# Inverting the triangles of a gated DeltaNet: 32-wide substitution against 16-wide substitution and one more block level

## The chip, the cores and the metric

The kernel runs on one core of a Trainium2 chip. The metric is the time of one execution in microseconds, as the device takes it. Of the kernel before there are three runs: 3832.81 us in the median, from 3832.29 to 3837.66.

## The reference

Two layers of a trunk run over 1024 latent and 256 context tokens of width 1024. In each, one input projection feeds three groups of heads: four gated DeltaNet (GDN) heads of width 128, run forwards and backwards over the tokens; a bidirectional linear recurrence (RG-LRU); and four heads of latent attention (MLA). One output projection and an MLP of squared ReLU follow. All data are fp32. The part that the change touches is in the GDN heads:

```python
def gdn_chunked(q, k, v, g, beta, s0):
    ...
    low = jnp.where(strict, jnp.einsum('nbhid,nbhjd->nbhij', kb, k) * decay, 0.0)
    amat = low + jnp.eye(GDN_CHUNK, dtype=low.dtype)
    rhs = jnp.concatenate([v * beta[..., None], kb * jnp.exp(G)[..., None]], axis=-1)
    sol = lax.linalg.triangular_solve(amat, rhs, left_side=True, lower=True, unit_diagonal=True)
    u, w = sol[..., :dv], sol[..., dv:]
    attn = jnp.einsum('nbhid,nbhjd->nbhij', q, k) * decay
    ...
    def step(S, inp):
        u_i, w_i, a_i, qg_i, kg_i, gl_i = inp
        v_new = u_i - jnp.einsum('bhcd,bhde->bhce', w_i, S)
        o_i = jnp.einsum('bhcd,bhde->bhce', qg_i, S) + jnp.einsum('bhij,bhje->bhie', a_i, v_new)
        S = S * gl_i[..., None, None] + jnp.einsum('bhcd,bhce->bhde', kg_i, v_new)
        return S, o_i
    S, o = lax.scan(step, s0, (u, w, attn, qg, kg, glast))
```

For every chunk of tokens a unit lower triangular matrix (`low` plus the identity) has to be solved. Only then can the scan, which goes from chunk to chunk, start.

## The kernel before

Tokens are kept along the free dimension, channels on the 128 partitions. Every large product of a weight and an activation is taken as three products of halves (high and low part of each, `mm3`, L230), 128 rows by up to 512 columns. The weights come by DMA as `wr` (SyncE's queue) and are split into `wh` (ScalarE) and `wl` = `wr` - `wh` (GpSimd, through the helper `tt`, L138). The helpers `act` (L135), `tt` (L138), `ts` and `stt` (L147) issue most other operations, so these lines stand for many places of the program; names of tiles tell them apart.

`mixer` writes the work of one layer in this order: `tiles(h)` for a head h (the projections to its k, q, v and z, with a convolution and a transposition, L443 and L462, behind each), `head(h)` (the GDN head), so that the projections of head h+1 are written behind head h, with a few tiles of the other groups between. After `head(2)` come the last projections, then `head(3)`; beside that one there is no projection left, and `mla_open`, `mla_prep` and `mla_attend` (the attention) and `lru` (the recurrence) are written behind it. What an engine does next is decided when the program is built: the Tile scheduler makes a list for each engine from the order of the program (the priority), the dependencies and its own estimates of times. So a part that gets shorter also changes which work stands between its instructions. At run time each engine goes through its list strictly in order, and waits on semaphores of the others.

The GDN head works with 10 chunks of 128 tokens (`NCH`) in two directions. `gdn_head` reads k, q and v back by DMA, forms the decays (L624, L636, L646) and the triangles `N[0]` and `N[1]`, each 128 x 10 x 128: minus the strictly triangular part, one lower, one upper. `gdn_invert` then inverts all 20 of them in place:

1. The four diagonal blocks of 32 x 32 of each triangle are brought together in `C` (128 x 20 x 32, four bands of partitions): direction 0 by four copies (L658), direction 1 transposed by 40 products with the identity on TensorE (L676) and a copy. `C` is filled up to 32 blocks with zeros by GpSimd (L668).
2. VectorE transposes in blocks of 32 (L681) to `X`, where each partition holds one whole 32 x 32 block along its free dimension, and sets the diagonal to one (L682).
3. The substitution: in 30 steps j, VectorE multiplies column j below the diagonal with row j left of it (`T`, r x j elements, r = 31 - j) and adds the product to `X`. That makes 60 operations on 9,920 elements per partition, each waiting for the one before. All blocks of a head are inverted at once, on 80 of 128 partitions.
4. Two block transposes (L689, L690) give the inverses back, as `X1` (in the place of `C`) and transposed as `X2`.
5. Two levels of block recursion on TensorE join 32 to 64 and 64 to 128 (products of L696, with copies between PSUM and SBUF that alternate between VectorE and ScalarE, `cp2`, L658).

`gdn_scan` follows (L766 to L790), then `gdn_y`, which scales the output on ScalarE and transposes it on TensorE (L821). `C`, `X` and `X2` are used again by the scan as buffers. PSUM is shared out in tags of one bank each: a, b and c serve the GDN head, d and st the convolutions and the attention, two banks of mm and one of lr the projections.

Of the kernel before, what the change touches and what calls it, by code (L numbers as in the profile page):

```python
# [7 lines left out]
F32 = mybir.dt.float32  # L8
# [3 lines left out]
ALU = mybir.AluOpType  # L12
# [4 lines left out]
P = 128  # L17
# [5 lines left out]
NCH = TOK // P  # L23
# [20 lines left out]
class Trunk:  # L44
# [615 lines left out]
    def gdn_invert(self, N):  # L660

        nc = self.nc
        C = self.g5("C")[:, 0:1024].rearrange("p (q i) -> p q i", i=32)
        X = self.g5("X")[:, 0:1024].rearrange("p (q i) -> p q i", i=32)
        X2 = self.g5("X2")[:, 0:1024].rearrange("p (q i) -> p q i", i=32)
        nc.gpsimd.memset(C[:, 2 * NCH:, :], 0.0)  # L668
        for a in range(4):
            q = slice(32 * a, 32 * a + 32)  # L670
            self.cp2(a, C[q, 0:NCH, :], N[0][q, :, 32 * a:32 * a + 32])
        pc = self.PT('a').rearrange("p (c i) -> p c i", i=32)
        for a in range(4):
            q = slice(32 * a, 32 * a + 32)
            for c in range(NCH):
                nc.tensor.matmul(pc[q, c, :], N[1][q, c, 32 * a:32 * a + 32], self.ident[q, 32 * a:32 * a + 32],  # L676
                                 start=True, stop=True, tile_position=(32 * a, 32 * a))
        self.act(C[:, NCH:2 * NCH, :], pc[:, 0:NCH, :])
        t = self.T()
        Xf = X.rearrange("p i j -> p (i j)")  # L680
        nc.vector.transpose(Xf, C.rearrange("p q i -> p i q"))  # L681
        nc.vector.memset(Xf[:, 0:1024:33], 1.0)  # L682
        for j in range(1, 31):
            r = 31 - j
            tv = t[:, 0:r * j].rearrange("p (i k) -> p i k", k=j)
            self.tt(tv, X[:, j + 1:32, j:j + 1].to_broadcast([P, r, j]), X[:, j:j + 1, 0:j].to_broadcast([P, r, j]), ALU.mult)
            self.tt(X[:, j + 1:32, 0:j], X[:, j + 1:32, 0:j], tv, ALU.add)
        X1 = C
        nc.vector.transpose(X1.rearrange("p q i -> p i q"), Xf)  # L689
        nc.vector.transpose(X2.rearrange("p q j -> p j q"), X.rearrange("p i j -> p j i"))  # L690
        Y = [[X1[:, 0:NCH], X2[:, 0:NCH]], [X2[:, NCH:2 * NCH], X1[:, NCH:2 * NCH]]]
        Q = [slice(32 * a, 32 * a + 32) for a in range(4)]
        H = [slice(0, 64), slice(64, 128)]

        def mm(out, lhsT, rhs, r, c):
            nc.tensor.matmul(out, lhsT, rhs, start=True, stop=True, tile_position=(r, c))  # L696

        pairs = [[(0, 1), (2, 3)], [(1, 0), (3, 2)]]
        pa = self.PT('b').rearrange("p (c i) -> p c i", i=32)
        for c in range(NCH):  # L700
            for d in range(2):
                for a, b in pairs[d]:
                    mm(pa[Q[b], c, :], N[d][Q[a], c, Q[b]], Y[d][1][Q[a], c, :], 32 * a, 32 * b)
        PT = self.T()[:, 0:320].rearrange("p (c i) -> p c i", i=32)
        self.act(PT, pa[:, 0:NCH, :])
        k = 0
        for d in range(2):
            for a in range(4):
                self.cp2(k, N[d][Q[a], :, Q[a]], Y[d][0][Q[a], :, :])
                k += 1  # L710
            for e in pairs[d][d]:
                self.cp2(k, self.XAT[Q[e], :, 32 * e - 64 * d:32 * e - 64 * d + 32], Y[d][1][Q[e], :, :])
                k += 1
        pw = self.PT('c').rearrange("p (c i) -> p c i", i=32)
        px = self.PT('a').rearrange("p (c i) -> p c i", i=32)
        for c in range(NCH):
            for d in range(2):
                for a, b in pairs[d]:
                    mm(pw[Q[a], c, :], PT[Q[b], c, :], Y[d][0][Q[b], c, :], 32 * b, 32 * a)
                a, b = pairs[d][d]  # L720
                mm(px[Q[b], c, :], Y[d][0][Q[b], c, :], PT[Q[b], c, :], 32 * b, 32 * b)
        for d in range(2):
            for a, b in pairs[d]:
                self.cp2(a, N[d][Q[a], :, Q[b]], pw[Q[a], 0:NCH, :])
            a, b = pairs[d][d]
            self.cp2(d, self.XAT[Q[b], :, 32 * a - 64 * d:32 * a - 64 * d + 32], px[Q[b], 0:NCH, :])

        for k in range(2):
            pb = self.PT('ab'[k]).rearrange("p (c i) -> p c i", i=64)
            for c in range(5 * k, 5 * k + 5):  # L730
                for d in range(2):
                    mm(pb[H[1 - d], c - 5 * k, :], N[d][H[d], c, H[1 - d]], self.XAT[H[d], c, :], 64 * d, 64 * (1 - d))
            PB = self.T()[:, 0:320].rearrange("p (c i) -> p c i", i=64)
            self.cp2(k, PB, pb[:, 0:5, :])
            pe = self.PT('cb'[k]).rearrange("p (c i) -> p c i", i=64)
            for c in range(5 * k, 5 * k + 5):
                for d in range(2):
                    mm(pe[H[d], c - 5 * k, :], PB[H[1 - d], c - 5 * k, :], N[d][H[1 - d], c, H[1 - d]], 64 * (1 - d), 64 * d)
            for d in range(2):
                self.cp2(d, N[d][H[d], 5 * k:5 * k + 5, H[1 - d]], pe[H[d], 0:5, :])  # L740

    def gdn_scan(self, h, gv, kT, ktd, vt, Y, at, Qg, last):

        nc = self.nc
        kt = self.g5("C").rearrange("p (c d) -> p c d", d=P)
        nc.sync.dma_start(kt, ktd.rearrange("p (c d) -> p c d", d=P))
        o = self.g5("X").rearrange("p (c d) -> p c d", d=P)
        sm = self.g5("X2").rearrange("p (k d) -> p k d", d=P)
# [189 lines left out]
    def mla_prep(self, L, h, mp, with_ctx):  # L938
# [35 lines left out]
        for b in qbl:  # L974
# [5 lines left out]
            for i in range(w):  # L980
                for j, b2 in enumerate(kb):
                    n2 = BLK[b2][1]
                    pm = self.G()[:, :n2]
                    nc.tensor.matmul(pm, a[0:96, 0, i * P:(i + 1) * P], K[b2][0:96, 0, :], start=True, stop=True)
                    nc.vector.tensor_reduce(mx[:, i, j:j + 1], pm, axis=AX.X, op=ALU.max)
            m1 = self.small([P, 4], "mx1", 2)
# [48 lines left out]
    def mixer(self, L, hs, obl):  # L1035

        nc = self.nc
# [6 lines left out]
        d = pk["krba"] = self.dram("krba")  # L1044
        ba = sp.tile([P, NCH, 16], F32, name=self.nm("ba"))
# [20 lines left out]
        gp = self.gp = self.pool("gp", other)  # L1066
        self.XAT = gp.tile([P, NCH, 64], F32, name=self.nm("XAT"))
        nc.gpsimd.memset(self.XAT, 0.0)
        kd, xg = [], []

        def tiles(h):
# [367 lines left out]
```

## Time and profile before

| what | value |
| --- | --- |
| median of the runs | 3832.81 us (3832.29 to 3837.66) |
| the profiled execution's own time | 3833.43 us |
| its span in the trace | 3831.6 us |
| instructions | 51,475 |
| TensorE's mean granted clock | 0.958 |
| ScalarE busy | 1645.2 us (43%) |
| GpSimd busy | 1310.3 us (34%) |
| moved by DMA | 347.13 MB, 91 GB/s |

The profile is of one execution. "Busy" is the time in which an engine executes something; PE is TensorE's matmuls, PEld its weight loads (which overlap), DVE VectorE, ACT ScalarE, POOL GpSimd. PEclk is the granted clock of TensorE as a share of full speed. A group's row names line, engine, operation, output and inputs, the shape, and behind "x" the count. A row of the timeline has start and duration in us, then the same, and in brackets the idle time ahead of it with what ended it. There are eight inversions, four per layer. By the trace they run, from the first block transpose to the first product after the substitution, from 174.4 to 219.4, 339.9 to 388.1, 485.5 to 525.4 and 630.5 to 691.5 us in layer 0, and from 2227.1 to 2273.4, 2379.7 to 2428.5, 2510.7 to 2559.9 and 2635.2 to 2696.2 us in layer 1.

### The profile page before, as it was taken

Reading aid. Unit: us, or ns where it says so; the run is one execution under the profiler, and the core shown is the slowest. Engines: PE = TensorE matmul, PEld = TensorE weight load, DVE = VectorE, ACT = ScalarE, POOL = GpSimd, SP = SyncE. Lnnn points to the kernel's source line nnn. Section 1 sums busy time; section 2 is a strip of 40 time slices with the busy share of each in tenths; the row PEclk is TensorE's granted clock in tenths of the full one; section 3 lists DMA queues with packets and bytes.
Section 4 is the critical chain, followed back from the end, with each engine's and each line's share of the span. In section 5 each row is a group of like instructions: output and inputs, shape, how many; then the busy total and the mean of one; then the engine's idle time right before and its main releaser. Section 6 shows DMA issues by size and latency. Waiting matters only on the chain. (4 is left out here: it accounts for less than half of the span.)

```text
span 3831.6 us, 51475 instructions
## 1 busy us (share of the span) xinstructions
PE 3501.0 (91%) x19236; PEld 2746.6 (72%) x19236; DVE 2093.5 (55%) x4351; ACT 1645.2 (43%) x3477; POOL 1310.3 (34%) x919
## 2 busy tenths in 40 slices
PE   5999986898999999999997989897887999999998
PEld 3777774645787888888877777774544778888886
DVE  6666577756365155555256685677766361421224
ACT  3554544545454322122354454554555453222242
POOL 4212212235575211111465322112244674222254
PEclk9999998899999999999998999997998999999999
DMA  5221213151532222222434322212002432311143
GB/s 184 93 92 60 93 60 93 34 161 44 175 105 89 66 83 94 88 94 89 130 107 138 99 81 78 86 65 74 31 27 81 153 105 94 96 47 47 51 139 99
DMA packets 164922, 347.13 MB, mean 91 GB/s; under 512 B 15552, under 2 KB 74304, under 8 KB 164672
## 3 DMA queue, kind: packets, MB, share of 16 engines
q1 hardware_dynamic: 164672, 343.85, 27.7%
q8 instruction: 151, 2.47, 0.3%
q14 instruction: 99, 0.81, 0.1%
HBM read 277.99 MB, written 65.80 MB: 90 GB/s over the span
## 5 line engine op out<-in xcount | busy, mean ns | idle before, releaser
L138 POOL TENSOR_TENSOR wl<-wr,wh 128x1024 fp32r<-128x1024 f32 x280 | 682.4, 2438 | 1630.0 <-ACT wh L135 951.7
L230 PE MATMUL mm<-A,wh 128*128 128x512 f32 (+1 forms) x3008 | 704.3, 377 | 11.8 <-DVE A L138 5.4
L135 ACT ACTIVATE wh<-wr 128x1024 fp32r<-128x1024 f32 x288 | 304.9, 1059 | 855.5 <-PE mm L230 332.5
L230 PEld LDWEIGHTS mm<-A,wh 128*128 128x128 f32 x3008 | 521.6, 193 | 107.2 <-DVE A L138 7.3
L138 DVE TENSOR_TENSOR hid<-T,hid 128x512 fp32r<-128x512 f32 (+1 forms) x160 | 172.4, 1080 | 451.9 <-ACT hid L135 451.9
L230 PE MATMUL mm<-A,wl 128*128 128x512 f32 (+1 forms) x1504 | 353.5, 371 | 1.2 <-DVE wl L138 1.1
L230 PE MATMUL mm<-hid,wh 128*128 128x512 f32 (+1 forms) x1280 | 301.8, 377 | 8.8 <-ACT T L135 6.8
L230 PEld LDWEIGHTS mm<-A,wl 128*128 128x128 f32 x1504 | 259.6, 191 | 48.1 <-DVE wl L138 1.3
L230 PEld LDWEIGHTS mm<-hid,wh 128*128 128x128 f32 x1280 | 227.3, 190 | 56.3 <-ACT T L135 7.3
L138 DVE TENSOR_TENSOR acc<-acc,mm 128x512 f32<-128x512 f32 (+1 forms) x140 | 88.5, 632 | 217.0 <-PE mm L230 216.4
L147 DVE SCALAR_TENSOR_TENSOR T<-raw,sm,T 128x512 f32<-128x512 f32 (+4 forms) x240 | 176.5, 737 | 47.8 <-ACT T L135 24.0
L230 PE MATMUL pd<-A,wh 128*128 128x512 f32 (+1 forms) x704 | 195.1, 406 | 0.0
L230 PE MATMUL plr<-A,wh 128*128 128x512 f32 (+1 forms) x800 | 185.7, 383 | 0.0
L1029 PE MATMUL pd<-Pt,V 128*128 128x512 f32 (+1 forms) x336 | 168.7, 627 | 16.9 <-ACT Pt L135 9.7
L135 ACT ACTIVATE T<-T 128x512 f32<-128x512 f32 (+1 forms) x243 | 141.6, 583 | 92.7 <-DVE T L147 69.8
L138 POOL TENSOR_TENSOR S<-S,T 128x512 f32<-128x512 f32 (+1 forms) x126 | 162.5, 1292 | 38.4 <-ACT T L135 35.3
L230 PE MATMUL mm<-hid,wl 128*128 128x512 f32 (+1 forms) x640 | 167.3, 379 | 8.1 <-DVE wl L138 8.1
L230 PE MATMUL pb<-A,wh 128*128 128x512 f32 (+1 forms) x800 | 173.0, 367 | 1.2 <-ACT wh L135 1.2
L147 DVE SCALAR_TENSOR_TENSOR ada<-wa,sil,ada 128x256 f32<-128x256 f32 x392 | 166.4, 488 | 6.6 <-DMA wa<-in_w_ada_dram 6.6
L230 PEld LDWEIGHTS plr<-A,wh 128*128 128x128 f32 x800 | 143.6, 188 | 31.8 <-issue 0.5
L230 PE MATMUL plr<-hid,wh 128*128 128x512 f32 (+1 forms) x640 | 155.8, 386 | 10.1 <-DVE hid L138 10.0
L147 DVE SCALAR_TENSOR_TENSOR lr<-lr,lr 128x256 f32<-128x256 f32 x218 | 108.3, 507 | 100.1 <-POOL lr L138 83.9
(382 smaller groups left out, 6822.5 us busy)
## 6 DMA issues: line engine op xcount, KB each, us to landing
wr<-in_w_mlp_dram SPq DMA_DIRECT2D x208, 512.0 KB, 3.5
wa<-in_w_ada_dram SPq DMA_DIRECT2D x96, 512.0 KB, 3.7
wr<-in_w_in_dram SPq DMA_DIRECT2D x48, 512.0 KB, 3.6
wr<-in_w_out_dram SPq DMA_DIRECT2D x32, 512.0 KB, 3.7
A<-y SPq DMA_DIRECT2D x32, 256.0 KB, 4.0
xm<-acc SPq DMA_DIRECT2D x32, 256.0 KB, 3.8
x<-xm SPq DMA_DIRECT2D x16, 512.0 KB, 6.4
kT<-k SPq DMA_DIRECT2D x8, 640.0 KB, 4.0
```

The costliest lines, as they stand in the source:

```text
L135: return self.nc.scalar.activation(out, in_, f, **kw)
L138: return (eng or self.nc.vector).tensor_tensor(out, a, b, op=op)
L147: return self.nc.vector.scalar_tensor_tensor(out, a, s, b, op0=op0, op1=op1)
L230: mm = nc.tensor.matmul(ps, w[wi][:, wk, :], a[:, ai, :], start=n == 0, stop=n == last)
L1029: nc.tensor.matmul(po, V[:, c, :], p, start=ci == 0, stop=ci == len(chunks) - 1)
```

## The change

The substitution works on blocks of 16 x 16, and a further level of the recursion joins 16 to 32.

Both diagonal 16 x 16 blocks of every 32 x 32 block are done in one operation: the second starts 528 elements behind the first (16 rows of 32 and 16 columns), so an access pattern of four dimensions covers both. That leaves 14 steps, 28 operations on 2,240 elements. The off-diagonal 16 x 16 square of each 32 block is cleared in `X` by GpSimd (L688), and taken from `C` before, as `V`, by two multiplications with a mask `up16` on GpSimd (128 x 320, one per direction), in buffers `t` and a new `t2`. After the two block transposes, TensorE forms three sets of 80 products of 32 x 32 (L702): V^T X2, to which VectorE adds the identity `i32` (the sum W goes to the place of `X`), then W^T X1 and X1^T W, which four copies (two VectorE, two ScalarE) bring back into `X1` and `X2`. Steps 1, 2 and 5 stay as they are. The two small constants are made once per layer by nine VectorE operations. All lines behind line 663 get higher numbers: what was L690 is L697, L696 is L702, L821 is L849, and so on.

```diff
         C = self.g5("C")[:, 0:1024].rearrange("p (q i) -> p q i", i=32)
-        X = self.g5("X")[:, 0:1024].rearrange("p (q i) -> p q i", i=32)
+        Xt = self.g5("X")
+        X = Xt[:, 0:1024].rearrange("p (q i) -> p q i", i=32)
...
-        t = self.T()
+
+        t, t2 = self.T(), self.T()
+        V = [v.rearrange("p (c i) -> p c i", i=32) for v in (t2[:, 0:320], t[:, 128:448])]
+        for d in range(2):
+            self.tt(V[d], C[:, d * NCH:(d + 1) * NCH, :], self.up16.to_broadcast([P, NCH, 32]), ALU.mult, nc.gpsimd)
         Xf = X.rearrange("p i j -> p (i j)")
         nc.vector.transpose(Xf, C.rearrange("p q i -> p i q"))
         nc.vector.memset(Xf[:, 0:1024:33], 1.0)
-        for j in range(1, 31):
-            r = 31 - j
-            tv = t[:, 0:r * j].rearrange("p (i k) -> p i k", k=j)
-            self.tt(tv, X[:, j + 1:32, j:j + 1].to_broadcast([P, r, j]), X[:, j:j + 1, 0:j].to_broadcast([P, r, j]), ALU.mult)
-            self.tt(X[:, j + 1:32, 0:j], X[:, j + 1:32, 0:j], tv, ALU.add)
+        nc.gpsimd.memset(X[:, 16:32, 0:16], 0.0)
+        B = Xt[:, 0:1056].rearrange("p (b s) -> p b s", s=528)[:, :, 0:512].rearrange("p b (i k) -> p b i k", k=32)
+        for j in range(1, 15):
+            r = 15 - j
+            tv = t[:, 0:2 * r * j].rearrange("p (b i k) -> p b i k", b=2, k=j)
+            self.tt(tv, B[:, :, j + 1:16, j:j + 1].to_broadcast([P, 2, r, j]), B[:, :, j:j + 1, 0:j].to_broadcast([P, 2, r, j]), ALU.mult)
+            self.tt(B[:, :, j + 1:16, 0:j], B[:, :, j + 1:16, 0:j], tv, ALU.add)
         X1 = C
         nc.vector.transpose(X1.rearrange("p q i -> p i q"), Xf)
         nc.vector.transpose(X2.rearrange("p q j -> p j q"), X.rearrange("p i j -> p j i"))
...
+        W = X[:, 0:2 * NCH, :]
+        for d in range(2):
+            dq = slice(d * NCH, (d + 1) * NCH)
+            pw = self.PT("bc"[d])[:, 0:320].rearrange("p (c i) -> p c i", i=32)
+            for c in range(NCH):
+                for q in Q:
+                    mm(pw[q, c, :], V[d][q, c, :], X2[q, d * NCH + c, :], q.start, q.start)
+            self.tt(W[:, dq, :], pw, self.i32.to_broadcast([P, NCH, 32]), ALU.add)
+        for d in range(2):
+            dq = slice(d * NCH, (d + 1) * NCH)
+            pf = self.PT("ac"[d])[:, 0:320].rearrange("p (c i) -> p c i", i=32)
+            pg = self.PT("ba"[d])[:, 0:320].rearrange("p (c i) -> p c i", i=32)
+            for c in range(NCH):
+                for q in Q:
+                    mm(pf[q, c, :], W[q, d * NCH + c, :], X1[q, d * NCH + c, :], q.start, q.start)
+            for c in range(NCH):
+                for q in Q:
+                    mm(pg[q, c, :], X1[q, d * NCH + c, :], W[q, d * NCH + c, :], q.start, q.start)
+            self.cp2(d, X1[:, dq, :], pf)
+            self.cp2(1 - d, X2[:, dq, :], pg)
...
+        self.i32 = gp.tile([P, 1, 32], F32, name=self.nm("i32"))
+        self.up16 = gp.tile([P, 1, 32], F32, name=self.nm("up16"))
+        nc.vector.memset(self.up16, 0.0)
+        for a in range(4):
+            q = slice(32 * a, 32 * a + 32)
+            nc.vector.tensor_copy(self.i32[q, 0, :], self.ident[q, q])
+            nc.vector.memset(self.up16[32 * a:32 * a + 16, :, 16:32], 1.0)
```

The scheduler also moves other work. Three places show it; each row has line, operation, output, inputs, shape and the semaphores waited for.

The first is VectorE's list at the end of the substitution of the first head of layer 0 (`T_1405` and `T_1416` are the buffer `t`; `raw`, `sm` and `T_2460` belong to a convolution of the next head, `hk` to its norms). Before:

```order
L138 TENSOR_TENSOR T_1405<-X_1356 128x58 [waits DVE_49]
L138 TENSOR_TENSOR X_1356<-X_1356,T_1405 128x2x29 [waits DVE_49]
L138 TENSOR_TENSOR T_1405<-X_1356 128x30 [waits DVE_49]
L138 TENSOR_TENSOR X_1356<-X_1356,T_1405 128x30 [waits DVE_49]
L689 STREAM_TRANSPOSE C_1355<-X_1356 128x32x32 [waits DVE_49]
L690 STREAM_TRANSPOSE X_251_1357<-X_1356 128x32x32
```

and after:

```order
L138 TENSOR_TENSOR X_1367<-X_1367,T_1416 128x2x14 [waits DVE_49]
L138 TENSOR_TENSOR hk_3179<-hk_3178,hk_3180 128x10 [waits DVE_49]
L696 STREAM_TRANSPOSE C_1366<-X_1367 128x32x32 [waits DVE_49,Pool_49]
L697 STREAM_TRANSPOSE X_253_1368<-X_1367 128x32x32
L147 SCALAR_TENSOR_TENSOR T_2460<-raw_2360,sm_84,T_2460 128x510 [waits DMAHW7_49,PE_49,Activation_49]
L138 TENSOR_TENSOR hk_3179<-hk_3179,hk_3178 128x10 [waits DVE_49]
L147 SCALAR_TENSOR_TENSOR T_2460<-raw_2360,sm_84,T_2460 128x511 [waits DVE_49]
L147 SCALAR_TENSOR_TENSOR hk_3178<-hk_3179,hk_3178 128x10 [waits DVE_49]
L138 TENSOR_TENSOR X_1367<-pb_1453,i_151_684 128x320 [waits PE_49]
```

Between the transposes and the first sum W stand two operations of a convolution and two of the norms. From the first block transpose to that of the end, other work takes 21, 24, 6, 24, 19, 18, 11 and 24 places of VectorE's list in the eight inversions, up to the first product; before it was 48, 49, 12, 54, 46, 46, 48 and 51.

The second place is TensorE's list in the same head, at the first products after the substitution (`pa`, `pb`, `pc` are PSUM banks; `mm` and `pd` those of projections). Before:

```order
L230 MATMUL mm_2401<-A_406,wl_2398 128x256
L230 MATMUL mm_2401<-A_410,wl_2398 128x256
L230 MATMUL mm_2401<-A_414,wl_2398 128x256
L696 MATMUL pb_1470<-X_251_1357,N_229_1231 32x32 [waits DVE_49]
L696 MATMUL pb_1470<-X_251_1357,N_229_1231 32x32
L696 MATMUL pb_1470<-C_1355,N_230_1232 32x32 x2
```

and after:

```order
L230 MATMUL pd_2419<-A_482,wh_2363 128x512
L702 MATMUL pb_1453<-X_253_1368,T_1417 32x32 [waits DVE_49,Pool_49]
L702 MATMUL pb_1453<-X_253_1368,T_1417 32x32 x39
L702 MATMUL pc_1495<-X_253_1368,T_1416 32x32 [waits PE_49,Pool_49]
L702 MATMUL pc_1495<-X_253_1368,T_1416 32x32 x39
L702 MATMUL pa_1537<-C_1366,X_1367 32x32 [waits DVE_49]
L702 MATMUL pa_1537<-C_1366,X_1367 32x32 x39
L702 MATMUL pb_1538<-X_1367,C_1366 32x32 [waits PE_49]
L702 MATMUL pb_1538<-X_1367,C_1366 32x32 x39
L702 MATMUL pc_1621<-C_1366,X_1367 32x32 [waits DVE_49]
L702 MATMUL pc_1621<-C_1366,X_1367 32x32 x23
```

The new products stand in one piece, without a projection between them, and the first of them comes about 110 rows of the list earlier than the first product of the old level did.

The third place is TensorE's list at the end of the third head of layer 1, where `gdn_y` transposes the output (L821, after L849; `gv` and `kT` belong to the fourth head, `wl_22657` and `wh_24116` to the last projections). Before:

```order
L230 MATMUL mm_22691<-A_17088,wl_22657 128x512
L230 MATMUL mm_22691<-A_17093,wl_22657 128x512
L636 MATMUL pc_22777<-kT_22753 128x128 [waits DMAHW7_49,DVE_49]
L636 MATMUL pc_22777<-kT_22753 128x128
L821 MATMUL pa_22156<-cst,X_21872 128x128 [waits Activation_49] x4
L821 MATMUL pb_22165<-cst,X_21872 128x128 [waits Activation_49] x3
L624 MATMUL pa_22765<-cst,gv_18174 128x128 [waits DVE_49]
```

and after:

```order
L230 MATMUL mm_24172<-A_17995,wh_24116 128x512
L230 MATMUL mm_24172<-A_18000,wh_24116 128x512
L849 MATMUL pa_23746<-cst,X_23462 128x128 [waits Activation_49]
L230 MATMUL mm_24172<-A_17965,wh_24116 128x512
L849 MATMUL pa_23746<-cst,X_23462 128x128 [waits Activation_49]
L230 MATMUL mm_24172<-A_17970,wh_24116 128x512
L849 MATMUL pa_23746<-cst,X_23462 128x128 [waits Activation_49] x2
L230 MATMUL mm_24172<-A_17975,wh_24116 128x512
L849 MATMUL pb_23755<-cst,X_23462 128x128 [waits Activation_49]
```

Before, the transposes follow the last projection matmuls; now projection matmuls stand ahead of them and between them.

More of the change, by code (lines that the diff above doesn't have):

```diff
@@ L690, in gdn_invert @@
         nc.vector.transpose(X2.rearrange("p q j -> p j q"), X.rearrange("p i j -> p j i"))
-        Y = [[X1[:, 0:NCH], X2[:, 0:NCH]], [X2[:, NCH:2 * NCH], X1[:, NCH:2 * NCH]]]
         Q = [slice(32 * a, 32 * a + 32) for a in range(4)]
-        H = [slice(0, 64), slice(64, 128)]
         def mm(out, lhsT, rhs, r, c):
             nc.tensor.matmul(out, lhsT, rhs, start=True, stop=True, tile_position=(r, c))
+        W = X[:, 0:2 * NCH, :]
[18 more added lines that the diff above has]
+            self.cp2(1 - d, X2[:, dq, :], pg)
+        Y = [[X1[:, 0:NCH], X2[:, 0:NCH]], [X2[:, NCH:2 * NCH], X1[:, NCH:2 * NCH]]]
+        H = [slice(0, 64), slice(64, 128)]
         pairs = [[(0, 1), (2, 3)], [(1, 0), (3, 2)]]
```

## The prediction

> **What bounds the kernel now.** I read the page's busy times and its chain first, then the table of stretches, then the waits of TensorE. The first line is the page's part 1 (busy us, share, instructions), the second the page's part 4 (shares of the chain that ended last).
>
> ```profile
> PE 3501.0 (91%) x19236; PEld 2746.6 (72%) x19236; DVE 2093.5 (55%) x4351; ACT 1645.2 (43%) x3477; POOL 1310.3 (34%) x919
> PE 19%; DVE 1%; issue 0%; POOLq 0%; DVEq 0%; ACT 0%; ACTq 0%
> ```
>
> TensorE is busy 91% of the span, and the chain that ended last runs through its matmuls; VectorE is busy 55%. Over the whole kernel, then, work taken from VectorE gains nothing by itself. What counts is the stage, so I cut out the eight inversions, from the first block transpose (L681) to the first product after the substitution (L696), and asked for TensorE's busy time in each.
>
> ```profile
> core 0: us, PE busy (x), PEclk, DMA share, GB/s
> 174.00:219.40 45.40, 39.16 (x208) 0.96 0.22 70
> 339.50:388.20 48.70, 39.53 (x215) 0.95 0.22 76
> 485.00:525.40 40.40, 30.83 (x156) 0.93 0.17 59
> 630.00:691.50 61.50, 34.96 (x94) 0.64 0.02 7
> 2227.00:2273.40 46.40, 38.57 (x188) 1.00 0.24 80
> 2379.00:2428.50 49.50, 41.57 (x193) 0.93 0.23 75
> 2510.00:2560.00 50.00, 42.66 (x211) 0.93 0.26 85
> 2635.00:2696.30 61.30, 37.90 (x103) 0.64 0.02 5
> ```
>
> There are two kinds of head. In six of them (heads 0 to 2 of each layer) TensorE is busy 76 to 86%, with the next head's input projections, and idle 6 to 10 us: 6.24 + 9.17 + 9.57 + 7.83 + 7.93 + 7.34 = 48 us in all. In the fourth head of each layer the projections are used up: it is idle 26.5 and 23.4 us, and its granted clock falls to 0.64. The wider stretches around that head name the engine that bounds it (columns: PE, PEld, DVE, ACT, POOL busy).
>
> ```profile
> core 0: us, PE busy (x) PEld busy (x) DVE busy (x) ACT busy (x) POOL busy (x), PEclk, DMA share, GB/s
> 620.00:700.00 80.00, 50.77 (x412) 31.16 (x414) 69.09 (x152) 31.25 (x70) 23.82 (x25) 0.70 0.07 20
> 700.00:760.00 60.00, 52.39 (x352) 40.55 (x351) 45.81 (x120) 36.68 (x117) 18.25 (x24) 0.91 0.07 21
> 2630.00:2700.00 70.00, 44.86 (x330) 26.85 (x329) 60.23 (x132) 25.17 (x54) 18.64 (x20) 0.67 0.02 5
> ```
>
> In the first and third stretch, around those inversions, VectorE is busy 86%, TensorE 63 and 64%. (The second holds the rest of that head's scan in layer 0.) In those two stages VectorE is the bound; in the other six heads TensorE is, and only waits on VectorE cost something.
>
> **The substitution: what goes from VectorE.** The two groups below are all multiplications and additions of the substitution, from the table of groups (busy us, mean ns).
>
> ```profile
> L138 DVE TENSOR_TENSOR T<-X 128x30 f32<-128x30 f32 (+14 forms) x240 | 103.7, 432 | 3.3
> L138 DVE TENSOR_TENSOR X<-X,T 128x30 f32<-128x30 f32 (+14 forms) x240 | 94.3, 393 | 3.0
> ```
>
> That is 198 us, 24.7 per head, but it holds stalls that will not go: the first two rows here are an addition in GpSimd and a multiplication in VectorE that overlaps it, from the timeline.
>
> ```profile
> 178.33 2.47 POOL L138 TENSOR_TENSOR wl<-wr,wh 128x1024 fp32r<-128x1024 f32 x1 [4.92 <-PE pd L230]
> 178.58 2.35 DVE L138 TENSOR_TENSOR T<-X 128x108 f32<-128x108 f32 x1
> 177.03 0.18 DVE L138 TENSOR_TENSOR T<-X 128x30 f32<-128x30 f32 x1
> 177.50 0.22 DVE L138 TENSOR_TENSOR T<-X 128x58 f32<-128x58 f32 x1
> 178.01 0.25 DVE L138 TENSOR_TENSOR T<-X 128x84 f32<-128x84 f32 x1
> 180.96 0.27 DVE L138 TENSOR_TENSOR X<-X,T 128x108 f32<-128x108 f32 x1
> 197.26 0.41 DVE L138 TENSOR_TENSOR X<-X,T 128x240 f32<-128x240 f32 x1
> ```
>
> The 108-element operation takes 2.35 us beside GpSimd's and 0.27 alone. GpSimd's work stays, so I count the operations without stalls: 0.18 us at 30 elements and 0.41 at 240 is 0.147 + 0.0011 per element, and dependent ones start some 0.035 later than they end. Before, 60 operations on 9,920 elements: 60 x 0.182 + 10.9 = 21.8 us. After, 28 operations on 2,240 elements (2 x r x j each, 28 to 112): 28 x 0.182 + 2.5 = 7.6 us. **14.2 us less per head.** That a fourth dimension in the access pattern costs more is nowhere in the trace; at twice the fixed part it would be 4 us, so 10 to 14.
>
> **What comes to VectorE.** Two additions that read PSUM (128x320) and two of the four copies out of PSUM of the same size.
>
> ```profile
> 227.09 0.49 DVE L658 COPY T<-pa 128x320 f32<-128x320 f32 x1 [0.25 <-PE pa L696]
> ```
>
> 4 x 0.49 = 2.0 us; the other two copies go to ScalarE, idle over half of these stages. **Net 12.2 us less per head.** Nine tiny set-up operations per layer (0.1 to 0.2 us each) I leave at nothing: they stand among others before the first projection is done; without that cover 1 us a layer.
>
> **What comes to TensorE.** 240 products of 32x32 in each head. Forty such products of the next step leave 80 records; the first stretch holds just these, of line L696 alone.
>
> ```profile
> core 0: us, PE busy (x) PEld busy (x), PEclk, DMA share, GB/s
> 219.00:220.15 1.15, 0.77 (x80) 0.77 (x80) 1.00 0.77 271
> 171.92 1.89 PE L676 MATMUL pa<-cst,N 32*32 32x32 f32 x62
> 191.69 3.89 PE L230 MATMUL pd<-A,wh 128*128 128x512 f32 x16
> ```
>
> 0.77 us per 40, so 240 cost **4.6 us**. L676's transposes, which stay on one block of the array for ten products, take 1.89 us for 31: 14.6 us for 240. The new loops change the block with every product, as L696 does; I take 4.6 and keep 14.6 as the far end. The Trainium skill ("TensorE: Matmul & The Clock Gate", section "Wait — 56ns, not 53.3ns?") says that small matmuls never start less than about 25 ns apart. By it the 480 records would take an estimated 12 us. This trace shows 9.6 ns (0.77 us over 80 records) on changing blocks, so here the measurement decides.
>
> The products also turn twice from PSUM to SBUF: sums W, then the results. One turn is 0.25 + 0.49 us and a start, about 1 us; with two directions one covers part of the other. I take 1.5 us of TensorE's idle time per head, between 0 and 4: the order puts no projection between these products, and VectorE has a few small operations queued ahead of each turn.
>
> **Six heads beside projections.** TensorE pays 4.6 + 1.5 = 6.1 us each. What comes back is idle time. These rows are its waits in the timeline, the last two at the tails of heads 1 and 2 in layer 1.
>
> ```profile
> 184.32 0.66 PE L443 MATMUL pst<-cst,T 128*128 128x128 f32 x4 [2.38 <-DVE T L147]
> 525.39 0.26 PE L696 MATMUL pb<-X,N 32*32 32x32 f32 x2 [9.57 <-DVE X L690]
> 2483.92 0.47 PE L821 MATMUL pa<-cst,X 128*128 128x128 f32 x1 [4.39 <-ACT X L135]
> 2611.82 1.35 PE L821 MATMUL pa<-cst,X 128*128 128x128 f32 x4 [5.45 <-ACT X L135]
> ```
>
> Transposes L443 wait 2.38 us for convolutions that share VectorE with the substitution, twice in most heads; in a run half as long one remains, so 2.3 us return. The wait at the end of the substitution (9.57 at worst) halves: 2 us a head. Net 6.1 - 4.3 = +1.8, six times **+11 us**. All idle gone would be 6 x 4.6 - 48 = -20; none gone +37. I stay near the middle, because the order moves the products forward to where VectorE will just be ready, as it did before.
>
> The tails: after, the order has 24 to 32 projection matmuls between the scan's end and the transposes of its output, at 3.89/16 = 0.24 us each some 6 us, so 4.39 + 5.45 = 9.8 us go; **-9 us**.
>
> **The fourth heads.** VectorE's 12.2 us come straight off the bound: **2 x -12.2 = -24 us**. TensorE's 6 us lie in its 25 idle ones. What is late next: the scan, which inherits the softmax maxima that the old order put beside the substitution; so the head does not gain the full shortening of its own chain. Bounds: half of 12.2 where the scan's chain of waits, not VectorE's load, sets its pace; all idle, 50 us together, where everything closes up.
>
> **GpSimd** gets two multiplications (320 elements) and a small fill per head.
>
> ```profile
> 172.14 1.27 POOL L138 TENSOR_TENSOR qT<-qT,T 128x512 f32<-128x512 f32 x1 [4.33 <-DMA k<-T]
> 2600.54 0.42 POOL L668 MEMSET C<- 128x384 f32 x1 [54.36 <-PE pb L780]
> ```
>
> By these, 2 x 0.85 + 0.4 = 2.1 us. The new waits: VectorE's first substitution step waits for GpSimd to give up a buffer, and convolutions are queued behind it; the second block transpose waits for the fill, long done by then. The weight split (178.33 above) is queued behind them, after 4.92 us of idle. I take nothing, at most 1 us per head. No DMA is added and SP's queue keeps its work.
>
> **Sum.** -24 + 11 - 9 = -22 us against the profiled execution's 3833.43 us, which stands 0.6 above the median: **3811 us**.
>
> **Rivals.**
> - *It closes up.* The fourth heads lose all 50 us of idle time (clock 0.64 speaks for more than VectorE's own time): 3833.4 - 50 + 11 - 9 = 3785. Against: VectorE has 12 us less, not 25. Chance 0.17.
> - *It does not shorten anything.* The scan of the fourth head takes the displaced work at its own pace and gives the 24 back; tails pay for the products: 3833.4 + 11 - 9 = 3835. For: VectorE is busy 45.81 of the 60 us after 700, 76%. Chance 0.17.
> - *TensorE pays.* In the six heads no idle time returns, since every wait on VectorE only moves into the scan: +37, tails unchanged, fourth heads -24: 3846. It decides from more than 24 us of cost in six heads, that is, less than 2.1 us of idle returned per head. Against: the 9.57 us wait must shrink. Chance 0.09.
> - *The products do not overlap*, as in L676: 10 us more in each of six heads, +60: 3871. The Trainium skill's 25 ns leans the same way. Against: the 80 records in 0.77 us, and the same alternation of blocks. Chance 0.05.
>
> Forecast: 0.52, its own range 3797 to 3824. The range runs to the first rival and takes in the second: 3780 to 3844, leaving out the last rival, most of the third and a little below. Within 0.2% (7.7 us, about what a measurement of this kernel can tell from no change): 0.17; faster 0.52 + 0.17 = 0.69; slower 0.14.
>
> **What would show it.** The fourth heads: stretch from the first block transpose to the first old product near 35 us instead of 61, the scan 8 to 15 longer. VectorE's total 90 to 100 us lower, TensorE's count up by 3,840 records. The new products 0.8 us per 80 records; 2.4 would mean the last rival. Idle of TensorE in the six heads near 30 us; at 48 the third is right. L821's two waits gone. Wrong altogether if VectorE's new operations take over 0.4 us each, or if GpSimd's two multiplications stall VectorE by their own length, 1.7 us a head.

## The result, and the profile after

The change makes the kernel slower: 3895.83 us in the median (3888.64 to 3903.27) against 3832.55 us (3831.67 to 3837.66), a ratio of 1.0162 with a 95% interval of 1.0141 to 1.0184. The prediction was 3811, with a range up to 3844: the sign was wrong. The span of the profiled execution went from 3831.6 to 3892.3 us.

The first line is the page's part 1 after the change, the second its chain, the third the row of part 3 for the queue that carries instructions (packets, MB).

```profile
PE 3543.2 (91%) x23076; PEld 2785.7 (72%) x23076; DVE 2037.0 (52%) x4145; ACT 1652.8 (42%) x3493; POOL 1330.1 (34%) x943
PE 21%; DVE 1%; issue 0%; ACT 0%; POOLq 0%; DVEq 0%; ACTq 0%
q8 instruction: 181, 2.97, 0.3%
```

VectorE is busy 56 us less (2093.5 to 2037.0). TensorE has 3840 matmul records and 3840 weight loads more, 42 us busy more, and the span grew by 61, so about 19 us of idle time came on top. The same queue had this row before:

```profile
q8 instruction: 151, 2.47, 0.3%
```

Thirty packets more, of 16,384 bytes each, for 7,680 TensorE instructions more: a packet holds 256 instructions.

The next rows are the eight inversions after the change, from the first block transpose to the first product of the old levels (columns: stretch, length, TensorE busy, granted clock), to be held against the eight rows in the prediction.

```profile
core 0: us, PE busy (x), PEclk, DMA share, GB/s
175.50:209.10 33.60, 23.76 (x560) 0.86 0.16 57
354.90:388.10 33.20, 23.66 (x563) 0.84 0.18 61
509.60:541.80 32.20, 21.64 (x551) 0.78 0.15 47
669.40:713.10 43.70, 17.51 (x488) 0.63 0.04 11
2270.20:2303.40 33.20, 22.99 (x553) 0.88 0.25 85
2432.30:2466.40 34.10, 24.59 (x551) 0.85 0.25 83
2567.70:2599.50 31.80, 22.84 (x556) 0.84 0.13 40
2697.40:2743.40 46.00, 19.64 (x489) 0.57 0.03 7
```

They are 8 to 18 us shorter, but TensorE is idle no less than before (9 to 11 us in the six heads, where it was 6 to 10, and 26 in the fourth), and its clock is lower: in the six heads 0.78 to 0.88 where it was 0.93 to 1.00. The table of TensorE's waits says why it is idle (line, waited for, us in total, times, longest):

```profile
PE pa L702 <- issue: 23.9, 15, 2.5
PE pb L702 <- DVE X L697: 21.4, 8, 5.8
PE pc L702 <- issue: 17.0, 9, 2.5
PE pst L443 <- DVE T L147: 16.3, 10, 2.4
PE pb L702 <- issue: 8.6, 7, 2.1
```

The waits "issue", 49.5 us, are new: TensorE stands in the middle of the 32x32 products, and no engine is named that it waits for. Before there were 1.8 us of that. The timeline of the first head shows them.

```profile
197.64 0.88 PE L702 MATMUL pb<-X,T 32*32 32x32 f32 x80 [1.61 <-DVE X L697]
198.37 0.88 PE L702 MATMUL pc<-X,T 32*32 32x32 f32 x80
199.39 0.52 PE L702 MATMUL pa<-C,X 32*32 32x32 f32 x36
201.67 0.55 PE L702 MATMUL pa<-C,X 32*32 32x32 f32 x42 [1.76 <-issue]
...
205.40 1.22 PE L702 MATMUL pc<-C,X 32*32 32x32 f32 x74 [2.44 <-issue]
...
208.85 0.47 PE L702 MATMUL pa<-X,C 32*32 32x32 f32 x18 [1.52 <-issue]
```

TensorE stops in the middle of a set (after 36 of 80 records of `pa`), so it is no operand and no bank that is missing. The single records of the trace, counted from pause to pause, beside the packets of the instruction queue:

```
TensorE's instructions since the last pause     stall            instruction packets (start, duration us)
392 (197.6 to 199.9)                            199.9, 1.76      199.35, 1.07
256 (201.7 to 203.0)                            203.0, 2.44      202.72, 1.24
256 (205.4 to 207.3)                            207.3, 1.52      206.44, 0.88
                                                                 209.96, 0.98
```

From one stall of over 0.9 us to the next of a run there are exactly 256 instructions, one packet (in four places 512, two packets); the first stall of a run came after 284 to 468 instructions in the eight heads. All 27 such stalls (47.7 us) end 1.2 to 1.6 us after a packet has landed, and while TensorE is short of them the packets follow each other at 3.3 to 4.1 us. One fp32 product of 32x32 is four instructions (two records of matmul and two weight loads), so a packet is 64 products: gone in 1.3 us at full clock, replaced in 3.5. The Trainium skill ("Runtime: NRT & Kernel Launch", section "Instruction fetch mechanics") says that instructions come in blocks of 16 KiB, 256 of them, and that crossing from one to the next is mostly hidden. The trace agrees with the block of 256; the crossing is hidden beside the large matmuls, and not in a run of 240 small products (27 stalls, 47.7 us).

A second loss comes with the first. The granted clock in parts of the same head (columns as above, with all engines):

```profile
core 0: us, PE busy (x) PEld busy (x) DVE busy (x) ACT busy (x) POOL busy (x), PEclk, DMA share, GB/s
201.60:203.00 1.40, 1.28 (x128) 1.18 (x128) 0.03 (x1) 0.03 (x1) 0.00 (x0) 1.00 0.06 12
205.40:207.30 1.90, 1.90 (x128) 1.79 (x128) 0.00 (x0) 0.00 (x0) 0.00 (x0) 0.50 0.03 9
209.40:212.00 2.60, 2.60 (x83) 1.84 (x79) 1.45 (x4) 2.31 (x5) 0.00 (x0) 0.50 0.02 6
```

128 records take 1.28 us at full clock and 1.90 at half; the clock comes back only at 213.6. In the six heads together TensorE was at half clock for 68 us before and for 112 us after.

### The profile page after: what moved, and what is told of

The parts are those of the page before. It is cut to its first block, busy times and chain, and to the rows that moved or that the text cites. A ratio compares the mean times of both kernels' runs of the same rounds, so it can differ in the third digit from the quotient of the medians.

```text
span 3892.3 us, 59034 instructions
## 1 busy us (share of the span) xinstructions
PE 3543.2 (91%) x23076; PEld 2785.7 (72%) x23076; DVE 2037.0 (52%) x4145; ACT 1652.8 (42%) x3493; POOL 1330.1 (34%) x943
## 3 DMA queue, kind: packets, MB, share of 16 engines
q1 hardware_dynamic: 164672, 343.85, 27.7%
## 5 line engine op out<-in xcount | busy, mean ns | idle before, releaser
L230 PE MATMUL mm<-A,wh 128*128 128x512 f32 (+1 forms) x3008 | 704.7, 376 | 11.7 <-DVE A L138 5.9
L230 PEld LDWEIGHTS mm<-A,wh 128*128 128x128 f32 x3008 | 518.9, 192 | 104.4 <-ACT A L135 7.9
L230 PE MATMUL mm<-A,wl 128*128 128x512 f32 (+1 forms) x1504 | 358.9, 372 | 1.5 <-DVE wl L138 1.4
L230 PE MATMUL mm<-hid,wh 128*128 128x512 f32 (+1 forms) x1280 | 302.9, 378 | 9.1 <-ACT T L135 6.8
L230 PEld LDWEIGHTS mm<-A,wl 128*128 128x128 f32 x1504 | 258.8, 190 | 46.9 <-DVE wl L138 1.6
L230 PEld LDWEIGHTS mm<-hid,wh 128*128 128x128 f32 x1280 | 227.8, 191 | 57.4 <-ACT T L135 7.2
L147 DVE SCALAR_TENSOR_TENSOR T<-raw,sm,T 128x512 f32<-128x512 f32 (+4 forms) x240 | 190.3, 794 | 64.3 <-ACT raw L135 32.3
L230 PE MATMUL pd<-A,wh 128*128 128x512 f32 (+1 forms) x704 | 191.3, 404 | 0.0
L230 PE MATMUL plr<-A,wh 128*128 128x512 f32 (+1 forms) x800 | 185.7, 383 | 0.0
L230 PE MATMUL mm<-hid,wl 128*128 128x512 f32 (+1 forms) x640 | 166.9, 379 | 8.1 <-DVE wl L138 8.1
L230 PE MATMUL pb<-A,wh 128*128 128x512 f32 (+1 forms) x800 | 171.5, 365 | 1.2 <-ACT wh L135 1.2
L230 PEld LDWEIGHTS plr<-A,wh 128*128 128x128 f32 x800 | 143.6, 188 | 31.7 <-issue 0.5
L230 PE MATMUL plr<-hid,wh 128*128 128x512 f32 (+1 forms) x640 | 153.5, 382 | 13.0 <-DVE hid L138 10.0
```

Of the source, the lines that this page charges most:

```text
L147: return self.nc.vector.scalar_tensor_tensor(out, a, s, b, op0=op0, op1=op1)
L230: mm = nc.tensor.matmul(ps, w[wi][:, wk, :], a[:, ai, :], start=n == 0, stop=n == last)
```

## The experiments

Two theories at the start. **A**: TensorE's instruction supply limits a long run of small products. **B**: the stalls are the turns between PSUM and SBUF, or come of the moved order. Beside them the question of the fourth heads. The table gives for each kernel the time from one inversion's first block transpose to the next one's, summed over the six heads that run beside projections (length = TensorE busy + idle), then the two stretches from a fourth inversion to the start of the output projection, the waits "issue" at products of 32x32 (those of the old levels included), and the time at half clock in the six heads; all from the profiled executions, in us.

| kernel | six heads | busy | idle | fourth stages | stalls "issue" | half clock |
| --- | --- | --- | --- | --- | --- | --- |
| before | 864 | 783 | 82 | 692 | 2 | 68 |
| after | 921 | 822 | 99 | 697 | 50 | 112 |
| only_fourth | 861 | 780 | 81 | 703 | 12 | 55 |
| only_first3 | 921 | 827 | 94 | 696 | 31 | 126 |
| products_alone | 950 | 831 | 119 | 715 | 52 | 154 |
| products_80 | 899 | 799 | 100 | 719 | 22 | 89 |
| spread | 908 | 839 | 69 | 698 | 16 | 74 |
| spread_80 | 907 | 821 | 86 | 699 | 30 | 74 |
| fewer | 893 | 809 | 84 | 688 | 31 | 89 |
| fewer_spread_80 | 884 | 811 | 73 | 689 | 22 | 84 |
| fewer_spread_40 | 866 | 804 | 63 | 688 | 10 | 53 |
| no_subst_fourth | 862 | 779 | 83 | 676 | 4 | 58 |
| no_subst_first3 | 821 | 771 | 50 | 703 | 4 | 24 |

A row is one execution and can lie some us beside the median: that of spread_80 was 6.6 us and that of fewer_spread_40 7.5 us under it.

### Which heads lose

```diff
-        self.gdn_invert(N)
+        (self.gdn_invert if h == 3 else self.gdn_invert32)(N)   # only_fourth; h < 3 in only_first3
```

`gdn_invert32` is the function of before.

> The new substitution and level only in the fourth head of each layer; the other six heads as before. The prediction's reason (VectorE is the bound beside the fourth heads): -24 us, about 3809. The theory from the trace after (the stretch from the fourth inversion to the output projection is as long as before, 363.3 against 358.5 us and 333.8 against 333.9, so another chain sets its end): within 8 us of before, 3832 to 3842.

Measured: 3838.29 us, ratio 1.0007 (0.9995 to 1.0019), as the theory from the trace had it.

> The new level in the first three heads of each layer, the fourth as before. If the fourth heads gain nothing and cost nothing, this takes nearly all of the loss: 3885 to 3895. If the fourth heads were worth the predicted 24 us, it is slower than the change itself, about 3920.

Measured: 3897.46 us, ratio 1.0155 (1.0140 to 1.0170), just above the first expectation and far from the second. So the whole loss lies in the six heads beside projections, and the fourth heads, the prediction's largest gain, give nothing.

### The products without the rest

```diff
 # in the kernel before, behind the two block transposes
+        for g in range(6):                       # range(2) in products_80
+            d = g % 2
+            pd = self.PT("bca"[g % 3])[:, 0:320].rearrange("p (c i) -> p c i", i=32)
+            for c in range(NCH):
+                for q in Q:
+                    mm(pd[q, c, :], X1[q, d * NCH + c, :], X2[q, d * NCH + c, :], q.start, q.start)
```

> The kernel before, with its 32-wide substitution, plus 240 products of 32x32 per head in one piece after the block transposes; nothing reads them, so no turn between PSUM and SBUF is added and VectorE saves nothing. Theory A (TensorE's instructions arrive in blocks of 256, one in about 3.5 us, and 240 products are 960 instructions): the same stalls without releaser as after the change, 1.5 to 2.5 us each, three or four per head, and 10 to 12 us per head in six heads: 3890 to 3910. Theory B (the stalls are the turns W and F, G, or the moved order): no such stalls, only the array's 5 us per head, 3855 to 3870.

Measured: 3944.16 us, ratio 1.0280 (1.0264 to 1.0295). No turn, no shorter substitution, and the same stalls, 52 us of them. That is A and not B. The loss is larger than A's numbers. I had counted six heads, and the fourth heads lose 23 us too; that the products lengthen a chain there, which no shorter substitution makes up for, is my reading and not shown. And 154 us at half clock, against 68, come with 48 us more of busy time in the six heads, where A had the array's 5 us per head.

> The kernel before plus 80 products of 32x32 per head in one piece (instead of the 240 that cost 108 us in all); nothing reads them. Theory A (instruction supply): 320 instructions are fewer than the 392 that ran before the first stall of the change, so no stall and no halved clock from it, only 1.5 us of the array per head: 3840 to 3852. Theory C (each product costs the same, whatever the number in a row, 108/240 of it): a third of 108 us, 3865 to 3875.

Measured: 3895.63 us, ratio 1.0155 (1.0136 to 1.0174). Neither expectation holds. The waits show why A's was wrong:

```profile
PE pb L696 <- issue: 17.3, 8, 2.4
PE pc L696 <- issue: 5.2, 5, 1.6
```

The 40 products of the old level (`pb` from `X` and `N`) follow the new ones at once, so the run is 120 products, 480 instructions, and each head stalls once or twice; the first stall came after 354 to 467 instructions. With the old levels behind them, 80 new products are already too long a run; fewer than 80 were not measured. That the fourth stages lose 27 us here, more than with 240 products, stays open.

### Holding the products apart

```diff
         self.cp2(1 - d, X2[:, dq, :], pg)
+        self.apart = {n0 + 3 * g: made[20 * g:20 * g + 20] for g in range(1, len(made) // 20)} if n0 else {}
+        self.nmm = 0
 # in mm3, behind each matmul of a projection
+                self.nmm += 1
+                for i in self.apart.pop(self.nmm, []):
+                    self.tc.add_manual_dep(i.ins, mm.ins.name, mybir.DependencyInfo(
+                        mybir.DependencyClass.NoSync, mybir.DependencyReason.DATA), reason="apart")
```

`made` lists the new products, and `n0` is the number of projection matmuls after which each head's first one stood anyway. In spread_80 it is `12 * g` and `80 * g`.

> The change, with the 240 products of heads 1 to 3 of each layer held apart: after every 20 of them three projection matmuls (0.24 us each) have to come first; the fourth heads are as in the change. Theory A (instruction supply): the stalls without releaser in those six heads go, some 6 us each, so 3850 to 3868. Theory B (turns and moved order): the turns are covered too, but the old levels and the scan start 5 us later and TensorE changes between small and large products 24 times per head: 3885 to 3905. The array's own time of the products, 5 us per head, stays in both.

Measured: 3884.95 us, ratio 1.0125 (1.0110 to 1.0140). The stalls went as A had it: from 50 us to 16, of which 12 lie in the fourth heads, as in the change. But the time misses A's range and stands at the edge of B's. Of 30 us of idle time that went in the six heads (99 to 69), 17 came back as busy time. The same 1661 projection matmuls of 512 columns and 624 of 256 between the inversions add 18.5 us more to TensorE's busy time than after the change (413.4 and 85.5 against 401.8 and 78.6 us). There are 66 more gaps between pieces, so 0.28 us each. In the timeline (L709 and L231 are L702 and L230 of the change):

```profile
203.30 0.55 PE L709 MATMUL pa<-C,X 32*32 32x32 f32 x40
203.78 0.62 PE L231 MATMUL mm<-A,wh 128*128 128x256 f32 x3
204.34 0.25 PE L709 MATMUL pb<-X,C 32*32 32x32 f32 x6
```

One round takes 1.04 us, for 40 records (0.39 at 9.6 ns) and three matmuls (0.37 at 0.122 us each). A's cause holds, but A left out the price of changing between small and large products, which B had named.

> The change, with the 240 products of heads 1 to 3 in three pieces of 80 and twelve projection matmuls between the pieces, instead of eleven times three matmuls. Theory A with the price of changing between small and large products (about 0.25 us per piece, from the run with pieces of 20): the stalls go nearly all and the changes cost 2 us per head less than in pieces of 20, 3855 to 3872. If it is the stretched chain (old levels and scan start later) that ate the gain of the pieces of 20, no better than those: 3880 to 3892.

Measured: 3887.30 us, ratio 1.0131 (1.0111 to 1.0152). The time falls into the second range, but not for its reason: against the pieces of 20, the six heads have 18 us less of busy time, as the price of changing would have it, and their stalls are back, 20 us instead of 4. Of the 30 us of stalls in all, 10 are in the fourth heads, 10 at the products of the old levels, which follow without a projection between, 6 inside the first piece of 80 (after 282 to 308 instructions) and 4 inside the later pieces. So 320 instructions in a row were already too many in three heads.

### Fewer products

```diff
-            for c in range(NCH):
-                for q in Q:
-                    mm(pg[q, c, :], X1[q, d * NCH + c, :], W[q, d * NCH + c, :], q.start, q.start)
-            self.cp2(d, X1[:, dq, :], pf)
-            self.cp2(1 - d, X2[:, dq, :], pg)
+            self.act(X1[:, dq, :], pf)
+            nc.vector.transpose(X2[:, dq, :], pf)
```

`X2` holds the transposes of `X1`'s blocks, and VectorE can transpose blocks of 32 straight out of PSUM; 160 products are left.

> The change without its third set of 80 products: X2 comes from a block transpose of W^T X1 on VectorE, straight from PSUM, in place of a product and a copy; 160 products in one piece. Theory A: 320 instructions less, that is 1.25 blocks of 3.5 us less per head, in six heads 26 us, and a little of the array and the clock: 3855 to 3872. Theory B (the turns set the time): the same number of turns and VectorE has more to do: 3888 to 3900.

Measured: 3854.84 us, ratio 1.0056 (1.0039 to 1.0073): 41 us less than the change, just below what A gave and far from B.

> Both: 160 products in heads 1 to 3 in two pieces of 80, twelve projection matmuls between. Theory A: no stalls; the array's own time of 160 products, 3 to 4 us in each of six heads, less some idle time that the shorter substitution gives back: 3838 to 3852, so about as fast as before or a little slower. Theory B: as the pieces of 20, 3875 to 3890.

Measured: 3845.39 us, ratio 1.0030 (1.0017 to 1.0044), in A's range, but in part by luck: A had no stalls, and 22 us of them are left, 16 in the six heads.

> 160 products in heads 1 to 3 in four pieces of 40, six projection matmuls between two pieces. Theory A: a piece of 40 with six matmuls needs 172 instructions in 2.2 us, 256 in 3.3, which is about what is supplied; the pieces of 80 needed 344 in 4.4 at first sight the same, but began with a full 320 at once and still stalled for 22 us in all. So the stalls fall to under 12 us, one more change of sizes per piece costs 0.25: 3830 to 3842. If the price of changing outweighs the stalls: 3845 to 3855.

Measured: 3833.97 us, ratio 0.9996 (0.9986 to 1.0006). The waits at the new products in this kernel:

```profile
PE pc L709 <- issue: 8.4, 8, 1.8
```

With 1.7 us more at the two other banks that is all of it, and the greater part (6.2 us) lies in the fourth heads, where nothing is put between. Time and stalls are both as A had them. The loss of the change is gone; a gain is not there either.

### What the substitution is worth

```diff
-        nc.vector.memset(Xf[:, 0:1024:33], 1.0)
-        for j in range(1, 31):
+        if h < 3:                                # h == 3 in no_subst_first3
+            nc.vector.memset(Xf[:, 0:1024:33], 1.0)
+        else:
+            nc.vector.memset(Xf, 0.0)
+        for j in range(1, 31 if h < 3 else 1):
```

> The kernel before, but in the fourth head of each layer the 30 steps of the substitution are left out and the diagonal blocks are set to zero; no product is added. It shows what VectorE's substitution is worth there at all. The prediction's reason (VectorE is the bound in these two stages): some 24 us of VectorE's work per head come off, about 3785. Theory D (the stage up to the output projection is bound by TensorE's attention work with its own waits; a shorter inversion only moves that work behind it): less than 10 us in all, 3824 to 3836.

Measured: 3816.00 us, ratio 0.9948 (0.9932 to 0.9965).

> The same in the first three heads of each layer, the fourth as before. It bounds what these six heads can gain from any shorter substitution, at no cost to TensorE. By the prediction's terms (4.3 us per head back for half of the substitution, 48 us of idle time at the most): 25 to 45 us faster, 3790 to 3810. If the waits of TensorE on VectorE only move elsewhere: less than 10 us, 3825 to 3836.

Measured: 3802.47 us, ratio 0.9908 (0.9894 to 0.9923), as the prediction's terms had it.

All of the substitution, some 25 us of VectorE's time in a head, is worth 10 us in a fourth head and 5.6 us in one of the six. For the fourth heads this lies between the two expectations: VectorE counts there, but for less than half of its time.

## Why the prediction was wrong

**What bounds each stage: half right.** That TensorE is the bound in six heads holds: taking the whole substitution away, some 148 us of VectorE's time, brings 34 us there. In the six heads the change costs 57 us of length (864 to 921), 40 of them busy and 17 idle.

**VectorE's part: right for the operations that the change touches.** The substitution's two groups took 198 us and now take these:

```profile
L138 DVE TENSOR_TENSOR T<-X 128x28 f32<-128x28 f32 (+6 forms) x112 | 41.4, 369 | 1.9
L138 DVE TENSOR_TENSOR X<-X,T 128x28 f32<-128x28 f32 (+6 forms) x112 | 40.4, 361 | 2.0
```

That is 116 us less, 14.5 per head, where 14.2 was forecast. The four added operations take 0.49 us each, as taken. But VectorE's whole busy time fell by 56 us, where 90 to 100 was named as the sign. The eight set-up copies, left at nothing, take 3.8 us, and the same 240 operations of the convolutions 13.8 us more, before and after:

```profile
L147 DVE SCALAR_TENSOR_TENSOR T<-raw,sm,T 128x512 f32<-128x512 f32 (+4 forms) x240 | 176.5, 737 | 47.8 <-ACT T L135 24.0
L147 DVE SCALAR_TENSOR_TENSOR T<-raw,sm,T 128x512 f32<-128x512 f32 (+4 forms) x240 | 190.3, 794 | 64.3 <-ACT raw L135 32.3
```

Why they got slower is open, and so is the rest.

**The step that failed: "240 cost 4.6 us".** It took the rate of 40 products between projections, 0.77 us, six times over. The array does keep it: the first 80 records after the change take 0.73 us from start to start. But 240 in a row need 960 instructions, and TensorE ran out of them after 284 to 468. From the first product to the first of the old levels it is 11.5 us in the first head (197.6 to 209.1) and 11.3 to 12.3 in the others, where 6.1 was forecast with the turns; 4.3 to 6.2 us of it are waits "issue". These waits are 50 us in all and the time at half clock rises by 43 us in the six heads, two terms that the sum did not have. The records of the 32x32 products add 31.9 us to TensorE's busy time in the six heads before and 73.3 after, which is all of the 40 us; the projections add no more than before (480 us against 482). At the forecast rate the new products are 28 of these 41 us; that the 13 left are the halved clock's is an estimate. The prediction had the number that matters on its page, 151 packets of instructions in 2.47 MB, and did not read it. Its fourth rival, "the products do not overlap", came nearest in size (3871) with another mechanism, one that does not happen: inside a run they overlap as before. The Trainium skill's 25 ns per small matmul ("TensorE: Matmul & The Clock Gate", section "Wait — 56ns, not 53.3ns?"), which the prediction set aside, gave an estimated 12 us. That this is about what was measured is luck: the records start some 9 ns apart at full clock (80 in 0.73 us), and the time is lost in the stalls and at half clock.

**Idle time returned: part of it, and spent.** The waits of the transposes L443 on the convolutions fell from 31.2 (15 times) to 16.3 (10 times), and the four waits of L821 on ScalarE, 16.6 us, are gone:

```profile
PE pst L443 <- DVE T L147: 31.2, 15, 4.0
PE pb L696 <- DVE X L690: 20.6, 7, 9.6
PE pa L821 <- ACT X L135: 16.6, 4, 6.3
```

(These are the rows of before.) The wait at the end of the substitution did not halve: 21.4 us after against 20.6. In the six heads, of 99 us of idle time after the change some 38 are stalls (50 less 12 in the fourth heads), so about 20 came back, against 35 forecast with the tails, and the stalls took them.

**The fourth heads: "VectorE's 12.2 us come straight off the bound" failed.** Forecast 24 us, measured none. The stretch in three pieces in layer 0, inversion, scan and the rest up to the output projection, before and after (columns as in the rows on the clock):

```profile
630.50:703.20 72.70, 43.46 (x382) 27.13 (x382) 64.03 (x140) 27.39 (x59) 21.89 (x25) 0.69 0.06 19
703.20:746.90 43.70, 38.43 (x233) 31.22 (x231) 35.05 (x88) 25.05 (x77) 10.87 (x14) 0.96 0.04 13
746.90:988.90 242.00, 217.23 (x750) 116.59 (x749) 156.17 (x285) 134.63 (x305) 104.82 (x137) 0.96 0.35 110
```

```profile
669.40:727.80 58.40, 30.75 (x792) 21.09 (x792) 48.26 (x92) 21.76 (x47) 22.17 (x26) 0.63 0.08 25
727.80:776.30 48.50, 45.74 (x270) 36.00 (x269) 31.38 (x83) 28.11 (x83) 9.07 (x14) 0.92 0.04 13
776.30:1032.70 256.40, 230.68 (x784) 120.96 (x782) 170.84 (x309) 138.11 (x314) 112.61 (x140) 0.95 0.34 104
```

The inversion got 14.3 us shorter. But TensorE did 12.7 us less beside it (43.46 to 30.75), and with it went attention work of VectorE (26 reductions for the maxima, `mx`, became 13); TensorE's idle time there stayed (29.2 and 27.7). The scan is 4.8 us longer and the rest 14.4. The prediction took VectorE, 86% busy for 70 to 80 us, for the bound of the stage; in the 242 us behind them TensorE is busy 90%, and what no longer fits beside the inversion is added there. The second rival ("it does not shorten anything") named this for the scan alone. The run without the substitution sets the size: 10 us per fourth head for all of it, so by estimate about 5 for half. That the new products and their 6 us of stalls per head took those 5 back is likely, but no run shows it alone.

**What stays open.** The six heads lose more in layer 0 (13.8, 9.1 and 14.8 us from one inversion to the next) than in layer 1 (9.5, 4.4 and 5.2); no run tells why. And how much of the loss is the halved clock alone was not separated by a run, and the 13 us above are an estimate. Nor does the lower clock come of the stalls alone: before the change there were 68 us of it with 2 us of stalls, and in the third head of layer 0 after it the clock was at half 2.4 us before the first new product, in a wait of 5.75 us for VectorE. Why a packet took 3.3 to 4.1 us to follow the one before is not shown either.

## What to carry to other kernels

Before many small products replace a few vector operations, count instructions as well as array time: here four for an fp32 product of 32x32, 256 in about 3.5 us, and an unbroken run of small products stalled after 220 to 530 instructions in the kernels measured; the granted clock fell with the stalls. If such products are needed, drop those that another engine can give (a block transpose out of PSUM), and put large matmuls between pieces that the supply can follow, not too often, for each such piece cost some 0.3 us here. And an engine that is the bound in a window need not be the bound of its stage: ask what work moves out of the window when it gets shorter, and who does it then.

## What the runs showed of the hardware that was not expected

TensorE's instructions came in packets of 16,384 bytes, 256 of them, one every 3.3 to 4.1 us while it was short, and it went on 1.2 to 1.6 us after each landing. In the kernel before, two waits of the same kind (1.8 us in all) stand at products of the old levels, so it met the same limit already. In the first head the granted clock fell to 0.5 some 3.4 us after the first stall began and stayed there for 10 us, the last 4 of them without a pause in the work. The Trainium skill ("TensorE: Matmul & The Clock Gate", section "HAM oscillation — how this bites in real kernels") gives idle gaps of over about 3.4 us as the rule for such a fall. In this head no gap was that long: in the 3.4 us before the fall TensorE was idle for 2.1, in a gap of 1.76 us and the start of one of 2.44.
